# A one-core hybrid encoder layer: PSUM scaling of q and k on VectorE, h stored as two parts, roots of the later blocks beside the gate/up products, larger early weight rings

## The chip, the core and the metric

The kernel runs on one core of a Trainium2 chip. The metric is the device time of one launch in microseconds; the time of a kernel is the median of its runs. The engines are PE (TensorE, matrix products), DVE (VectorE), ACT (ScalarE), POOL (GpSimd) and SP (SyncE). SP issues nearly all DMA transfers, and it does so in the order of its queue: a transfer whose data are not ready holds up all transfers behind it.

## The reference

One layer over 2048 prompt rows and 8 streams of 16 rows (2176 rows in all), model width 1024, FFN width 2816, all in float32:

```python
h = _rmsnorm(x, norm1_g) * (1 + scale) + shift
z = h @ w_in                                  # 1024 -> 2568 columns
u_a, u_g, q, k, v, f = jnp.split(z, ...)
u = u_a * jax.nn.sigmoid(u_g)
q = _rmsnorm(q.reshape(b, t, N_HEADS, HEAD_DIM), q_norm_g)
k = _rmsnorm(k.reshape(b, t, N_HEADS, HEAD_DIM), k_norm_g)
logf = jax.nn.log_sigmoid(f + b_f)
...
attn = softmax(q k / 8 + cum[q] - cum[k], causal) @ v
conv_out = silu(layernorm(causal_depthwise_conv31(u) + conv_b))
x = x + g1 * (concat(conv_out, attn) @ w_out)
h = _rmsnorm(x, norm2_g) * (1 + sc2) + sh2
x = x + g2 * ((jax.nn.silu(h @ w_gate) * (h @ w_up)) @ w_down)
```

The outputs are x, the normed k, v, logf and the last convolution rows.

## The kernel before

Activations lie with channels on the 128 partitions and rows of the sequence along the free axis. A float32 product is made from parts: each factor is split into a high part (rounded to the fp32r format by ACT, "Copy") and a low part (the factor less its high part, a subtraction on DVE or POOL), and PE runs three matmuls, high with high, low with high, high with low. So each operand of a product costs an ACT pass and a subtraction, and a tile is ready for PE when both are done.

The program is written as Python code for each stage, and a planner of the framework puts the instructions of each engine into a fixed order by a simulation of its own. All engines then run their own lists in order and wait for each other by semaphores. A list that is ordered badly for the real durations stands still behind the instruction that waits.

The stages that the change touches:

- **u and v** (`project_u_v`, blocks of 384 rows). `h_block` makes the normed input h for a block: for each of 8 channel tiles SP loads xT, POOL multiplies by the root (L464), ACT scales and shifts (L466), SP writes h to memory (`h_d`, L471), ACT and POOL make its parts `hh` and `hl` (L472, L473). Three buffers hold h, 16 each hold the parts.
- **q and k** (`project_q_k`). For each block, `load` reads h back and makes its parts a second time (L501 to L503). `product` makes 8 products of 24 matmuls (L514), 4 for q and 4 for k; ACT copies each out of PSUM and squares it. `finish` for the block before is woven in, one step per product: the head sums, a root by Newton steps on DVE (L94 to L96), and then for each of 8 tiles a matmul that spreads the root over the channels (`R`, L549), and the scaled q or k. For rows below `LATE = 1536` ACT scales R by the gain (L553) and POOL multiplies (L554); for later rows DVE does both in one instruction that reads R from PSUM (L556). Then the parts of the result are made on ACT (L559) and POOL (L560) and written out by SP (`q_d`, `k_d`, `o_k`, L563 to L566).
- Beside it run the depthwise convolution (`conv_taps`, 31 taps, L706 on DVE, 7 chunks of rows) and the remaining modulation vectors (`ada_rest`: a load `wa` into a single buffer, L266, matmuls L271, then L279 on DVE). A chunk of the convolution accumulates in two PSUM banks (`cv`) up to row 1536, and in SBUF (`ca`) for the later chunks.
- **Attention** follows, with the last of the finishing work, the convolution's normalization and the sample streams.
- **Output projection** (`project_out`, 6 blocks of 360 or 368 rows). For each block 8 tiles `cr` are loaded (three buffers), split into `ch` (ACT) and `cl` (POOL, L1141) and multiplied with w_out (L1124) into 8 PSUM banks; `scaled_add` adds the result to x; the squares are summed in `ssum` on POOL. `root` takes the root of the mean of squares: four matmuls (L1171), a chain of 16 short DVE instructions, four matmuls (L1180), an ACT copy. The root of a block is taken in the block after; those of blocks 2 to 5 are written to `r_d`. After block 2, `norm(0)` makes the normed inputs of the first pair of blocks: 16 multiplies on POOL (L1245), 16 on ACT (L1247), sums and differences on DVE (L1285), and writes to `ht_d`.
- **Gate/up and down products** (`ffn_up`, `ffn_down`). A scheme of seven products per pair of blocks takes the place of eight. Weights W and right sides T go through rings of slots: raw weights `rR` (512 columns each), split weights `rW`, split right sides `rT`. For the first pair of blocks the sums of weights are made on DVE (L1352) as well. `pump` issues loads and splits until the rings are full; `rings` opens small rings (8 T, 4 W, 4 R) before the output projection, `grow` opens the rest after it (R 11, W 6, T 13 and 9). A product takes four T and one W: 12 matmuls (L1424). `norms` makes the normed inputs of pairs 1 and 2 beside the products of pair 0, one step after every second product. PSUM banks go round in the order of `BANK8`, where bank `ss` is every eighth.

Of the kernel before, what the change touches and what calls it, by code (L numbers as in the profile page):

```python
# [43 lines left out]
LATE = 1536  # L44
# [74 lines left out]
class Layer:  # L119
# [30 lines left out]
    def run(self, stop=99):  # L150
# [3 lines left out]
        with ExitStack() as ctx:  # L154
# [5 lines left out]
            self.h_d = d.tile([P, CB, TT], F32, name="h_d")  # L160
# [269 lines left out]
    def h_block(self, b0, b1, xp, sp, hp, ep=None):  # L430
# [44 lines left out]

    def project_q_k(self):
# [49 lines left out]
        def finish(b0, b1, zs, ss, sqs, tag):  # L526
# [16 lines left out]
            for g in range(NP):  # L543
                for w in range(2):
# [7 lines left out]
                    if b0 < LATE:  # L552
                        nc.scalar.activation(y[:, :n], R, AF.Copy, scale=self.gain[:, w, g:g + 1])  # L553
                        nc.gpsimd.tensor_tensor(y[:, :n], zs[w][g][:, :n], y[:, :n], ALU.mult)  # L554
                    else:
                        nc.vector.scalar_tensor_tensor(y[:, :n], zs[w][g][:, :n], self.gain[:, w, g:g + 1], R, ALU.mult, ALU.mult)  # L556
# [119 lines left out]
    def conv_taps(self, ch):  # L676
# [5 lines left out]
        for jp in range(2):  # L682
# [468 lines left out]
    def project_out(self, ctx):  # L1151
# [3 lines left out]
        ones = sp.tile([P, P], F32, name="ones2")  # L1155
        nc.vector.memset(ones, 1.0)
        mean = sp.tile([P, 2], F32, name="mean2")
        nc.vector.memset(mean, 1.0 / D)
        ident = sp.tile([P, P], F32, name="ident2")
        nc.sync.dma_start(ident, a["ident"])  # L1160
# [478 lines left out]
```

## Time and profile before

| what | value |
|---|---|
| median of 3 runs | 2921.28 us (2919.7 to 2922.06) |
| the profiled execution | 2918.41 us, of which 2916.6 us is the span from its first to its last instruction |
| mean granted TensorE clock | 0.965 |
| PE busy | 2743.4 us, 94% of the span |
| DVE busy | 2163.8 us, 74% |
| ACT, POOL busy | 1469.7 us (50%), 681.7 us (23%) |
| DMA | 585.43 MB, mean 201 GB/s |

The profile counts an engine as busy from the start to the end of its instructions. A line of a table of stretches gives for each engine the busy time and, in brackets, the number of instructions, then the clock that was granted to TensorE (1.00 is full speed), the share of time that the 16 DMA engines were busy, and GB/s. In a list of groups the last two numbers before the second bar are the total busy time and the mean ns of one instruction. "[14.77 <-DMA wa<-w_ada]" behind an instruction says that its engine stood idle for 14.77 us before it, until that transfer landed. A row with "x32" merges 32 instructions, and its second number is then the time from the start of the first to the end of the last.

### The profile page before, as it was taken

What the parts mean: (1) busy time and instruction counts of PE and PEld (TensorE: products, weight loads), DVE (VectorE), ACT (ScalarE), POOL (GpSimd) and SP (SyncE); (2) the same over time, 40 slices, a digit from 0 to 9 for tenths busy, and PEclk for the clock granted to TensorE, in tenths of its full rate; (3) what the DMA queues carried; (4) which work ended last, traced back from release to release, by engine and by line L of the source; (5) the groups of instructions that cost most, each with busy time, mean ns of one, the idle gap of its engine ahead of it and who ended that gap; (6) DMA issues with size and microseconds to landing.
All of it is one profiled execution on the core that took longest, in us unless ns stands there. A gap on an engine that the chain in (4) does not pass through costs nothing.

```text
span 2916.6 us, 48768 instructions
## 1 busy us (share of the span) xinstructions
PE 2743.4 (94%) x16536; PEld 2530.6 (87%) x16536; DVE 2163.8 (74%) x4155; ACT 1469.7 (50%) x2892; POOL 681.7 (23%) x813
## 2 busy tenths in 40 slices
PE   7999989789899899989879999999999999999999
PEld 6999967666566677779878999999999999999999
DVE  3698988878778677742349999877797778676765
ACT  4533424346676667764335444544454446555553
POOL 3555555553222223225524200000000000000000
PEclk9999999898998999999989999999999999999999
DMA  8643536464333866453638877867696678888883
GB/s 300 223 132 110 163 122 193 137 186 133 95 94 113 193 191 186 146 179 124 218 124 287 299 246 233 276 216 224 219 314 201 207 226 274 266 258 270 271 261 116
DMA packets 377738, 585.43 MB, mean 201 GB/s; under 512 B 46240, under 2 KB 236864, under 8 KB 375440
## 3 DMA queue, kind: packets, MB, share of 16 engines
q1 hardware_dynamic: 363024, 556.89, 59.6%
q0 software_dynamic: 14464, 25.42, 3.7%
q8 instruction: 131, 2.15, 0.3%
q14 instruction: 119, 0.97, 0.1%
HBM read 413.05 MB, written 169.16 MB: 200 GB/s over the span
## 4 chain that ended last, share of the span: by engine, by line
PE 55%; DVE 4%; DMA 3%; ACT 1%; issue 1%; POOL 1%; SPq 0%; DVEq 0%; POOLq 0%; ACTq 0%
PE z L1424 41%; PE acc L1124 6%; PE pv L948 3%; PE s L957 1%; PE s L958 1%; DVE rW L1141 1%; PE mx L918 1%; PE lane L1087 1%; DVE rR L1352 1%; DMA nx<-x_d 1%; POOL nx L1245 1%; DMA rR<-w_up 1%; PE lane L1053 1%; DMA vraw<-o_v 0%; PE pr L1180 0%
## 5 line engine op out<-in xcount | busy, mean ns | idle before, releaser
L1424 PE MATMUL z<-rT,rW 128*128 128x360 f32 (+1 forms) x8316 | 1379.2, 328 | 19.1 <-ACT rW L1140 15.6
L1424 PEld LDWEIGHTS z<-rT,rW 128*128 128x128 f32 x8316 | 1376.5, 188 | 21.3 <-ACT rW L1140 17.0
L1140 ACT ACTIVATE rW<-rR 128x512 fp32r<-128x512 f32 x714 | 433.7, 616 | 373.5 <-PE z L1424 272.3
L1141 DVE TENSOR_TENSOR rW<-rR,rW 128x512 fp32r<-128x512 f32 x714 | 482.2, 680 | 140.0 <-ACT rW L1140 135.5
L948 PE MATMUL pv<-e,V 128*128 128x512 f32 (+3 forms) x960 | 268.3, 384 | 3.9 <-DVE e L1141 1.1
L706 DVE SCALAR_TENSOR_TENSOR cv<-cu,cpar,cv 128x384 f32<-128x384 f32 x464 | 248.8, 614 | 4.7 <-ACT cv L704 4.4
L921 DVE TENSOR_REDUCE M<-mx 128x1 f32<-128x512 f32 (+2 forms) x320 | 189.3, 604 | 62.2 <-PE mx L918 41.8
L962 ACT ACTIVATE ef<-s 128x512 f32<-128x512 f32 (+3 forms) x320 | 165.9, 531 | 120.2 <-PE s L958 43.5
L948 PEld LDWEIGHTS pv<-e,V 128*128 128x128 f32 x960 | 169.7, 194 | 52.5 <-DVE e L1141 6.1
L1141 POOL TENSOR_TENSOR e<-ef,e 128x512 fp32r<-128x512 f32 (+3 forms) x106 | 126.6, 1194 | 376.3 <-ACT e L1140 179.6
L1141 DVE TENSOR_TENSOR rT<-traw,rT 128x360 fp32r<-128x360 f32 (+1 forms) x315 | 160.0, 540 | 68.9 <-ACT rT L1140 68.7
L1140 ACT ACTIVATE rT<-traw 128x360 fp32r<-128x360 f32 (+1 forms) x315 | 148.7, 501 | 93.6 <-DMA traw<-gt_d 71.4
L1141 DVE TENSOR_TENSOR e<-ef,e 128x512 fp32r<-128x512 f32 (+3 forms) x214 | 151.2, 714 | 43.4 <-ACT e L1140 42.0
L1140 ACT ACTIVATE e<-ef 128x512 fp32r<-128x512 f32 (+3 forms) x320 | 174.4, 566 | 5.4 <-PE pv L948 1.0
L918 PE MATMUL mx<-K,Q 96*128 96x512 f32 (+2 forms) x320 | 135.5, 431 | 15.0 <-DVE M L921 14.5
L1124 PE MATMUL acc<-ch,woh 128*128 128x360 f32 (+1 forms) x384 | 128.5, 337 | 12.6 <-ACT ch L1140 10.4
L706 DVE SCALAR_TENSOR_TENSOR ca<-cu,cpar,ca 128x384 f32<-128x384 f32 (+1 forms) x232 | 125.6, 611 | 12.8 <-ACT ca L704 12.7
L514 PE MATMUL z<-hqh,wqh 128*128 128x384 f32 (+1 forms) x384 | 132.3, 345 | 1.3 <-ACT sq L518 1.1
L1352 DVE TENSOR_TENSOR rR<-rR 128x512 f32<-128x512 f32 (+1 forms) x136 | 93.1, 700 | 52.2 <-DMA rR<-w_down 40.1
L957 PE MATMUL s<-Q,K 128*128 128x512 f32 (+3 forms) x320 | 128.5, 403 | 2.5 <-ACT ef L962 2.3
L1124 PE MATMUL acc<-cl,woh 128*128 128x360 f32 (+1 forms) x384 | 120.5, 338 | 10.2 <-POOL cl L1141 10.2
L514 PE MATMUL z<-hql,wqh 128*128 128x384 f32 (+1 forms) x384 | 128.7, 336 | 0.0
(318 smaller groups left out, 4511.7 us busy)
## 6 DMA issues: line engine op xcount, KB each, us to landing
rR<-sup_d SPq DMA_DIRECT2D x176, 256.0 KB
rR<-w_gate SPq DMA_DIRECT2D x132, 256.0 KB
traw<-gt_d SPq DMA_DIRECT2D x154, 180.0 KB
rR<-w_down SPq DMA_DIRECT2D x104, 256.0 KB
rR<-sdn_d SPq DMA_DIRECT2D x96, 256.0 KB
rR<-w_up SPq DMA_DIRECT2D x88, 256.0 KB
sup_d<-rR SPq DMA_DIRECT2D x88, 256.0 KB
wa<-w_ada SPq DMA_DIRECT2D x16, 1024.0 KB
```

The source lines that it names most:

```text
L514: nc.tensor.matmul(z[:, :n], w[:, m], x[:, :n], start=(c == 0 and k == 0), stop=(c == CB - 1 and k == 2))
L706: self.pin(nc.vector.scalar_tensor_tensor(dst, src, w, acc[i], ALU.mult, ALU.add))
L918: nc.tensor.matmul(mx[:, :w], Q2[0:AUX, h, j * P:(j + 1) * P], K2[kb][0:AUX, h, :w], start=True, stop=not diag)
L921: nc.vector.tensor_reduce(M[:, i, kb:kb + 1], mx[:, :w], AX.X, ALU.max)
L948: nc.tensor.matmul(z[h][:, off:], V[kt // 4][:, v, kt % 4, h:h + 2, :].rearrange("p b c -> p (b c)"), e[:, x, off:], start=(kt == 0 and i ...
L957: nc.tensor.matmul(s[:, off:], K1[kb][:, h, sl], Q1[:, h, off:], start=True, stop=False)
L962: nc.scalar.activation(ef[:, off:], s[:, off:], AF.Exp)
L1124: self.nc.tensor.matmul(z[:, :n], w[:, m], y, start=(first and i == 0 and k == 0), stop=(last and i == len(terms) - 1 and k == 2))
L1140: self.nc.scalar.activation(hi, raw, AF.Copy)
L1141: engine.tensor_tensor(lo, raw, f32(hi), ALU.subtract)
L1352: nc.vector.tensor_tensor(t, x, y, op)
L1424: nc.tensor.matmul(z, W[:, x, m], t[:, y, :w], start=(k == 0 and i == 0), stop=(k == n - 1 and i == 2))
```

## The change

1. DVE scales every tile of q and k out of PSUM in one instruction; the branch with ACT and POOL is gone.
2. `h_d` holds both parts of h, so the q and k stage loads them ready to use; the write waits for the low part, and twice as many bytes go each way.
3. The chunk of the convolution that ends at row 1920 accumulates in PSUM as well.
4. In the output projection the low parts `cl` are made by DVE, `cr` has four buffers, and `pump` is called once before the last block.
5. `root` becomes a method that two stages call. For blocks 2 to 5 the output projection writes the sums of squares to `r_d`, and `norms` takes the root beside the gate/up products, in PSUM bank `ss`.
6. The early rings are larger (W 6, R 12); the sum is W 10 as before, R 15 as before, T 29 (30 before).

```diff
-LATE = 1536
...
-            self.h_d = d.tile([P, CB, TT], F32, name="h_d")
+            self.h_d = d.tile([P, CB, 2, TT], F32, name="h_d")
...
-            hl = hp.tile([P, NB], F32R, tag="hl", name="hl")
-            hh = hp.tile([P, NB], F32R, tag="hh", name="hh")
+            hx = hp.tile([P, 2, NB], F32R, tag="hx", name="hx")
+            hh, hl = hx[:, 0], hx[:, 1]
...
-            nc.sync.dma_start(self.h_d[:, c, b0:b1], h[:, :n])
             nc.scalar.activation(hh[:, :n], h[:, :n], AF.Copy)
             nc.gpsimd.tensor_tensor(hl[:, :n], h[:, :n], f32(hh[:, :n]), ALU.subtract)
+            nc.sync.dma_start(self.h_d[:, c, :, b0:b1], f32(hx[:, :, :n]))
             yield hh, hl
...
-                h = hp.tile([P, NB], F32, tag="h", name="hq", bufs=3)
-                nc.sync.dma_start(h[:, :n], self.h_d[:, c, b0:b1])
-                nc.scalar.activation(hh[:, :n], h[:, :n], AF.Copy)
-                nc.gpsimd.tensor_tensor(hl[:, :n], h[:, :n], f32(hh[:, :n]), ALU.subtract)
-                hs.append((hh, hl))
+                hx = hp.tile([P, 2, NB], F32R, tag="hx", name="hqx")
+                nc.sync.dma_start(f32(hx[:, :, :n]), self.h_d[:, c, :, b0:b1])
+                hs.append((hx[:, 0], hx[:, 1]))
...
-                    if b0 < LATE:
-                        nc.scalar.activation(y[:, :n], R, AF.Copy, scale=self.gain[:, w, g:g + 1])
-                        nc.gpsimd.tensor_tensor(y[:, :n], zs[w][g][:, :n], y[:, :n], ALU.mult)
-                    else:
-                        nc.vector.scalar_tensor_tensor(y[:, :n], zs[w][g][:, :n], self.gain[:, w, g:g + 1], R, ALU.mult, ALU.mult)
+                    nc.vector.scalar_tensor_tensor(y[:, :n], zs[w][g][:, :n], self.gain[:, w, g:g + 1], R, ALU.mult, ALU.mult)
...
-            if c1 <= 1536:
+            if c1 <= 1920:
                 acc = [shaped(self.bank("cv", "cv")) for _ in range(2)]
...
-                raw = cp.tile([P, NW], F32, tag="cr", name="cr")[:, :n]
+                raw = cp.tile([P, NW], F32, tag="cr", name="cr", bufs=4)[:, :n]
...
-                self.parts_of(hh, hl, raw, nc.gpsimd)
+                self.parts_of(hh, hl, raw, nc.vector)
...
-            if b1 == TT:
-                self.pump()
...
-            if pending:
-                R = root(*pending)
-                if bi < 3:
-                    first.append(R)
-                if bi == 2:
-                    drain(self.norm(0, sp, lambda k, h: xs01[h][k], first))
+            if 0 < bi < 3:
+                first.append(self.root(*pending, sp))
+            if bi == 2:
+                drain(self.norm(0, sp, lambda k, h: xs01[h][k], first))
             if bi < 2:
                 xs01 = (xs01 if bi else []) + [xs]
-            pending = (bi, ssum)
-        root(*pending)
+                pending = (ssum, n)
+            else:
+                nc.sync.dma_start(self.r_d[bi, :, :n], ssum[:, :n])
+            if bi == len(HALVES) - 2:
+                self.pump()
...
-                r = pool.tile([P, NW], F32, tag="nR", name="nR", bufs=2)
-                nc.sync.dma_start(r[:, :n], self.r_d[2 * p + h, :, :n])
-                R.append(r)
+                s = pool.tile([P, NW], F32, tag="ns", name="ns", bufs=1)
+                nc.sync.dma_start(s[:, :n], self.r_d[2 * p + h, :, :n])
+                R.append(self.root(s, n, pool))
+                yield
...
-        for k, n in (("T", 8), ("W", 4), ("R", 4)):
+        for k, n in (("T", 8), ("W", 6), ("R", 12)):
...
-        for k, n, side in (("R", 11, None), ("W", 6, "right"), ("T", 13, "right"), ("T", 9, None)):
+        for k, n, side in (("W", 4, "right"), ("T", 16, "right"), ("R", 3, None), ("T", 5, None)):
```

The body of `root` is as before; its constants now live in a pool of their own that `rings` opens.

Because the planner orders the engines anew, the places that matter are shown as the lists have them. The lines after the change have other numbers (L706 is L697, L1141 is L1132, L1424 is L1412, L1171 and L1180 are L1203 and L1212).

First DVE in the q and k stage, while the chunk of rows 1536 to 1920 is convolved (`ca` and `cv` are its accumulators, `qn` the scaled q or k, `mod` the modulation vectors). Before:

```order
L706 SCALAR_TENSOR_TENSOR ca<-cu,cpar,ca 128x384 x2
L282 TENSOR_SCALAR mod_108<-mod_108,n2T 128x9
L706 SCALAR_TENSOR_TENSOR ca<-cu,cpar,ca 128x384 x32
L279 TENSOR_SCALAR mod_106<-pm_4967,bT 128x9
L279 TENSOR_SCALAR mod_107<-pm_4967,bT 128x9
```

After:

```order
L697 SCALAR_TENSOR_TENSOR cv<-cu,cpar,cv 128x384 x7
L547 SCALAR_TENSOR_TENSOR qn<-zs,gain,R 128x384
L697 SCALAR_TENSOR_TENSOR cv<-cu,cpar,cv 128x384 x8
L547 SCALAR_TENSOR_TENSOR qn<-zs,gain,R 128x384
L697 SCALAR_TENSOR_TENSOR cv<-cu,cpar,cv 128x384 x9
L547 SCALAR_TENSOR_TENSOR qn<-zs,gain,R 128x384
```

The run of 32 convolution steps without a break is cut into runs of 8 with one `qn` between, and its accumulator is in PSUM.

Then PE at the start of the gate/up products (`acc` is the last block of the output projection, `z` the gate/up products, 12 matmuls each, `pr` the two matmul groups of a root). Before:

```order
L1124 MATMUL acc<-cl,woh 128x360
L1424 MATMUL z<-rT,rW 128x368 x30
L1171 MATMUL pr<-mean_13543,ssum 90x2 x4
L1424 MATMUL z<-rT,rW 128x368 x18
L1180 MATMUL pr<-odg,ones_13541 128x90 x4
L1171 MATMUL pr<-mean_13543,ssum 90x2 x4
L1180 MATMUL pr<-odg,ones_13541 128x90 x4
L1424 MATMUL z<-rT,rW 128x368 x1800
```

After:

```order
L1115 MATMUL acc<-cl,woh 128x360
L1412 MATMUL z<-rT,rW 128x368 x264
L1203 MATMUL pr<-sp_13266,ns 90x2 x4
L1412 MATMUL z<-rT,rW 128x368 x72
L1212 MATMUL pr<-odg,sp_13265 128x90 x4
L1203 MATMUL pr<-sp_13266,ns 90x2 x4
L1212 MATMUL pr<-odg,sp_13265 128x90 x4
L1412 MATMUL z<-rT,rW 128x368 x372
L1203 MATMUL pr<-sp_13266,ns 90x2 x4
L1412 MATMUL z<-rT,rW 128x368 x90
```

The root of block 4 and that of block 5 stood 30 and 48 matmuls into the gate/up products; now 22 products come first, then the root of block 2, with 6 products between its two groups, and right behind it the root of block 3 with nothing between; those of blocks 4 and 5 follow further down with products between.

DVE at the same place (`xo` is x after the projection, `rT` and `rW` the low parts of right sides and weights, `rR` sums of weights, `ov`, `or`, `ot` and `odg` the chain of a root, `e` and `eU` the first results that are taken out of the gate/up products). Before:

```order
L1141 TENSOR_TENSOR rT<-traw,rT 128x368
L1136 TENSOR_TENSOR xo<-xo,acc 128x128
L1141 TENSOR_TENSOR rT<-traw,rT 128x368 x8
L1173 TENSOR_SCALAR ov<-pr 90x4
L1141 TENSOR_TENSOR rT<-traw,rT 128x368
L1174 TENSOR_SCALAR or<-ov 90x4
L1141 TENSOR_TENSOR rT<-traw,rT 128x368
L1175 TENSOR_SCALAR or<-or 90x4
L1141 TENSOR_TENSOR rT<-traw,rT 128x368
L94 SCALAR_TENSOR_TENSOR ot<-or 90x4
L1141 TENSOR_TENSOR rT<-traw,rT 128x368
L95 TENSOR_TENSOR ot<-ot,ov 90x4
```

After:

```order
L1123 SCALAR_TENSOR_TENSOR xo<-acc,mod_106,xo 128x232
L1127 TENSOR_TENSOR xo<-xo,acc 128x128
L1340 TENSOR_TENSOR rR<-rR 128x512 x3
L1126 TENSOR_TENSOR acc<-acc,mod_106 128x128
L1132 TENSOR_TENSOR rW<-rR,rW 128x512
L1340 TENSOR_TENSOR rR<-rR 128x512
L1132 TENSOR_TENSOR rW<-rR,rW 128x512
L1132 TENSOR_TENSOR rT<-traw,rT 128x368 x3
L1127 TENSOR_TENSOR xo<-xo,acc 128x128
L1132 TENSOR_TENSOR rT<-traw,rT 128x368 x3
L1132 TENSOR_TENSOR rW<-rR,rW 128x512 x6
L1132 TENSOR_TENSOR rT<-traw,rT 128x368 x4
```

The low parts of right sides were alternated with a root's chain and no weight was made; now sums and low parts of weights alternate with right sides, and of the first weights six are made ahead of the last `xo` where it was four.

Last SP in the u and v stage, where the parts of h are made for a block (`h` is the tile that xT is loaded into). Before:

```order
L345 DMA o_v<-v 128x252
L471 DMA h_d<-h 128x384 x2
L345 DMA o_v<-v 128x260
L463 DMA h<-xT 128x384
L345 DMA o_v<-v 128x252
L463 DMA h<-xT 128x384 x2
L471 DMA h_d<-h 128x384 x3
```

After:

```order
L344 DMA o_v<-v 128x252
L437 DMA x<-x 128x1024 x2
L344 DMA o_v<-v 128x260
L344 DMA o_v<-v 128x252
L472 DMA h_d<-hx 128x2x384
L462 DMA h<-xT 128x384
L472 DMA h_d<-hx 128x2x384
```

Writes and loads went in groups of up to three; now each load of the next tile stands behind a write that waits for a low part.

More of the change, by code (lines that the diff above doesn't have):

```diff
@@ L1154, in project_out @@
         sp = ctx.enter_context(self.pool(name="osp", bufs=1))
[L1155 to L1160, printed above, removed]
         self.tables("silu_and_others", self.last_exp)
@@ L1163, in project_out @@
         W = {}
-        def root(bi, ssum):
-            n = HALVES[bi][1] - HALVES[bi][0]
-            m = n // 4
-            pr = self.bank("ss", "pr")
-            for i in range(4):
-                nc.tensor.matmul(pr[:m, 2 * i:2 * i + 2], ssum[:, i * m:(i + 1) * m], mean, start=True, stop=True)
-            v, r, t = (sp.tile([P, 4], F32, tag=k, name="o" + k)[:m] for k in "vrt")
-            nc.vector.tensor_scalar(v, pr[:m, 0:8:2], EPS, None, ALU.add)
-            nc.vector.tensor_scalar(r.bitcast(I32), v.bitcast(I32), 1, None, ALU.arith_shift_right)
-            nc.vector.tensor_scalar(r.bitcast(I32), r.bitcast(I32), -1, 0x5F3759DF, ALU.mult, ALU.add)
-            newton_rsqrt(nc, r, t, v, 3)
-            for i in range(4):
-                dg = sp.tile([P, NW // 4], F32, tag="dg", name="odg", bufs=4)[:m, :m]
-                nc.vector.tensor_scalar(dg, ident[:m, :m], r[:, i:i + 1], None, ALU.mult)
-                nc.tensor.matmul(pr[:, i * m:(i + 1) * m], ones[:m], dg, start=True, stop=True)
-            R = sp.tile([P, NW], F32, tag="R", name="oR", bufs=2)
-            nc.scalar.copy(R[:, :n], pr[:, :n])
-            if bi < 2:
-                return R
-            nc.sync.dma_start(self.r_d[bi, :, :n], R[:, :n])
         pending, first = None, []
@@ L1291, in rings @@
         self.count = dict.fromkeys("TWR", 0)
-        for k, n in (("T", 8), ("W", 4), ("R", 4)):
+        for k, n in (("T", 8), ("W", 6), ("R", 12)):
             self.slots(ctx, k, n)
+        cp = ctx.enter_context(self.pool(name="spread", bufs=1))
+        self.spread = ones, mean, ident = [cp.tile([P, k], F32, name=f"sp{i}") for i, k in enumerate((P, 2, P))]
+        self.nc.vector.memset(ones, 1.0)
+        self.nc.vector.memset(mean, 1.0 / D)
+        self.nc.sync.dma_start(ident, self.a["ident"])
         self.tr = ctx.enter_context(self.pool(name="traw", bufs=6))
```

20 lines of the change are left out of this document (18 added, 2 removed).

## The prediction

> **What bounds the kernel now.** I read the table of stretches first, cut where PE changes its work: u and v, q and k, attention, output projection, start of the gate/up products, the rest.
>
> ```profile
> 0.00:344.30 344.30, 319.62 (x2304) 311.50 (x2305) 252.50 (x518) 142.89 (x264) 166.87 (x323) 0.98 0.56 183
> 344.30:645.30 301.00, 260.04 (x1498) 217.29 (x1496) 257.81 (x544) 120.50 (x257) 179.82 (x179) 0.94 0.54 161
> 645.30:1271.80 626.50, 573.07 (x3173) 416.18 (x3172) 467.05 (x809) 428.47 (x859) 177.48 (x175) 0.93 0.50 143
> 1271.80:1500.40 228.60, 205.50 (x1216) 203.59 (x1217) 78.25 (x175) 91.58 (x172) 101.71 (x103) 0.94 0.52 170
> 1500.40:1713.40 213.00, 186.40 (x1090) 183.55 (x1089) 191.94 (x373) 100.06 (x196) 55.81 (x36) 0.93 0.81 274
> 1713.40:2916.60 1203.20, 1198.74 (x7260) 1198.48 (x7260) 916.23 (x1741) 586.15 (x1147) 0.00 (x0) 1.00 0.75 239
> ```
>
> PE (first pair of numbers) is the bound nearly everywhere. The last row has no gap, and nothing in the change makes its matmuls fewer. What can be won are the gaps of the rows between: 41 us in q and k, 23 in the output projection, 27 at the start of gate/up, and the slow clock behind each gap. So next I read what PE waited for there.
>
> ```profile
> PE pm L271 <- DMA wa<-w_ada: 16.3, 2, 14.8
> PE R L549 <- DVE mod L279: 11.4, 3, 6.2
> PE acc L1124 <- ACT ch L1140: 10.4, 2, 8.3
> PE acc L1124 <- POOL cl L1141: 10.2, 2, 5.8
> PE ssq L523 <- ACT sq L518: 10.0, 2, 8.7
> ```
>
> The longest wait names a DMA; the timeline tells why that transfer was late.
>
> ```profile
> 411.33 17.02 DVE L706 SCALAR_TENSOR_TENSOR ca<-cu,cpar,ca 128x384 f32<-128x384 f32 x32
> 412.02 17.18 POOL L560 TENSOR_TENSOR qp<-qn,qp 128x384 fp32r<-128x384 f32 x1 [0.64 <-ACT qp L559]
> 430.65 0.54 SPq L266 DMA_DIRECT2D wa<-w_ada  x1
> 437.98 1.94 PE L271 MATMUL pm<-wa,sT 128*32 128x512 f32 x8 [14.77 <-DMA wa<-w_ada]
> 522.52 13.70 POOL L554 TENSOR_TENSOR qn<-zs,qn 128x384 f32<-128x384 f32 x1 [4.72 <-ACT qn L553]
> 536.25 0.52 ACT L559 ACTIVATE qp<-qn 128x384 fp32r<-128x384 f32 x1 [13.81 <-POOL qn L554]
> ```
>
> While DVE ran 32 convolution steps with all operands in SBUF, one POOL subtraction took 17.18 us; SP stood behind it with the writes of q, and the load `wa` behind those. At 522 the same befell L554, ACT stood behind it, and PE behind ACT's squares (the 8.7 us).
>
> **Scaling on DVE, and one more chunk in PSUM.** The rows for the prices:
>
> ```profile
> L560 POOL TENSOR_TENSOR qp<-qn,qp 128x384 fp32r<-128x384 f32 (+1 forms) x48 | 70.9, 1478 | 65.7 <-ACT qp L559 65.6
> L554 POOL TENSOR_TENSOR qn<-zs,qn 128x384 f32<-128x384 f32 x32 | 57.2, 1788 | 46.3 <-ACT qn L553 46.2
> L556 DVE SCALAR_TENSOR_TENSOR qn<-zs,gain,R 128x384 f32<-128x384 f32 (+1 forms) x16 | 8.6, 540 | 9.2 <-DMA o_k<-qn 4.9 <-POOL qp L560 2.7 <-PE R L549 0.9
> 392.00:453.00 61.00, 35.73 (x58) 0.86 0.44 141
> 453.00:505.00 52.00, 45.39 (x52) 1.00 0.68 206
> 173.28 7.44 DVE L706 SCALAR_TENSOR_TENSOR cv<-cu,cpar,cv 128x384 f32<-128x384 f32 x14
> 360.00:422.90 62.90, 53.51 (x291) 49.57 (x289) 1.00 0.38 128
> ```
>
> The two stretches in the middle count the convolution (L706) alone, the last one the matmuls L514. DVE gains 32 instructions of 0.540 us, 17.3 us. The moved chunk took 35.73 + 45.39 = 81.1 us for 110 steps; into PSUM a step takes 7.44/14 = 0.53 us, so 58.3, 22.8 less. DVE's sum goes from 257.8 to 252.3 us in a stretch of 301. PE without waits made 291 matmuls in 62.9 us, 0.216 each; 960 of that size and 192 of 256 columns (two thirds each, estimated) are 235 us, and some 10 for the first attention matmuls in the last block: 245. Both engines thus want about 250, and each waits for the other once per product (R for DVE, banks for PE). I add a tenth, 275: **26 us won**. Ends: 255 (46 won) if they never wait, 301 (none) if DVE's rows, now 4.8 us per product with one `qn` behind 8 steps, hold PE's R banks each time. POOL's 57.2 us go, and its L560 waits at most for a run of 8 steps in PSUM. The later chunks, 128 columns wide, stay in SBUF, in runs of up to 16 between two `qn`: short stops of POOL remain.
>
> **Parts of h stored.** In q and k, 48 ACT copies and 48 POOL subtractions go; PE's list names them with 0.3 us only, so I give nothing for them beyond the above. Each way 128 x 8 x 2176 x 4 bytes, 8.9 MB, are added: 30 GB/s on 161 in q and k, where the DMA engines are busy 54% of the time, hidden. In u and v it is 26 on 183. There the first block's 1.6 MB come while weights are awaited; at 300 GB/s (slice 1 of the page) they last 5 us. I take 2 lost, ends 0 and 5, and nearer the low end since the writes stand behind the loads in SP's order.
>
> **Output projection.** The rows:
>
> ```profile
> 1280.00:1500.40 220.40, 200.06 (x1152) 196.84 (x1152) 0.95 0.52 169
> 1400.25 8.97 POOL L1245 TENSOR_TENSOR xo<-xo,oR 128x368 f32<-128x368 f32 x8 [3.04 <-ACT oR L1182]
> 1410.47 2.77 PE L1124 MATMUL acc<-cl,woh 128*128 128x360 f32 x8 [5.84 <-POOL cl L1141]
> 1404.66 1.30 DVE L1285 TENSOR_TENSOR ot<-xo 128x368 f32<-128x368 f32 x1
> 1414.71 0.53 DVE L1285 TENSOR_TENSOR ot<-xo 128x368 f32<-128x368 f32 x1
> 1418.76 0.91 SPq L1199 DMA_DIRECT2D cr<-cat_d  x2
> L1180 PE MATMUL pr<-odg,ones 90*128 90x90 f32 (+1 forms) x48 | 8.2, 327 | 7.3 <-DVE odg L1179 7.3
> L1171 PE MATMUL pr<-mean,ssum 128*90 128x2 f32 (+1 forms) x48 | 5.0, 226 | 0.6 <-ACT oR L1182 0.6
> ```
>
> 1152 matmuls at 1198.74/7260 = 0.165 us are 190 us; 220 were spent. PE stood behind POOL's `cl` for 10.2 us, because 8 multiplies `xo` stood ahead of it. Then a `cr` load stood on SP behind the writes of `ht_d` until 1418.76. The first stop goes with `cl` on DVE, which is busy 78 us of 228.6 here and takes on 48 x 0.54 = 26 us; the second goes by the fourth buffer and the order, in which block 3's tiles are loaded ahead of the writes. Slow clock behind both, about 4. The root of block 2 and that of block 3 leave: (8.2 + 5.0)/6 = 2.2 us of PE each. And ACT makes the first `ch` ahead of four copies `rW`, 4 x 0.62 = 2. In all 10 + 3 + 4 + 4 + 2 = 23, less 7 for stops that the new order brings: **16 us won**, ends 3 (only the roots) and 23. The summing on POOL stays and is off PE's path; if it ran late it would hold `ssum`, and so the root of the next block only.
>
> A rule of the Trainium skill speaks here. The row first: DVE's L1285 took 1.30 us beside POOL's multiplies and 0.53 without. The Trainium skill (SBUF — State Buffer, section "Who interferes with whom") states that a DVE instruction with two inputs in SBUF contends with a POOL instruction that reads SBUF, and that one of them blocks fully. By that, 411 to 428 us was such a stop and PSUM accumulators end it, but `cl` on DVE is now one more such instruction beside `xo` and `ssum`. That is the second rival.
>
> **Roots beside gate/up, more weights ready.**
>
> ```profile
> 1500.40:1550.00 49.60, 20.47 (x101) 18.88 (x102) 0.69 0.66 214
> 1550.00:1650.00 100.00, 100.00 (x601) 100.00 (x601) 1.00 0.90 306
> 1650.00:1713.40 63.40, 59.98 (x357) 59.12 (x356) 1.00 0.80 269
> 1516.32 1.37 PE pr L1171 x8
> 1520.36 2.03 PE pr L1180 x8
> 1522.41 0.47 ACT oR L1182
> 1523.26 4.46 DMA rR<-w_up
> ```
>
> These stretches count L1424 alone, the four rows below are from the chain of waits. 1059 matmuls at 100/601 = 0.166 are 176 us; 213 passed. Two roots stood in line, then the load of `w_up` began only at 1523. Now six weights and 12 raw ones are there before, so 8 T and 6 W carry PE over the first 6 products at least in W, and no root comes before product 22. What is late next: DVE, 191.9 us busy of 213. It gains two roots, 2 x 16 x 0.2 = 6.4, and loses two `rW` and four `rR`, 2 x 0.68 + 4 x 0.70 = 4.2 (0.68 and 0.70 from the groups of L1141 and L1352): 194. PE needs 176, four roots of 2.2, and for block 3's root, which has nothing between its groups, DVE's chain from 1517.69 to 1520.36, 2.7, and ACT's 0.47: 188. DVE is the bound; with 6 for waits 200: **13 us won**, ends 3 and 19. One T less ahead costs nothing, since behind 1713 PE never waited for T.
>
> **The sum.** 26 + 16 + 13 - 2 = 53. The profiled execution took 2918.4, so 2865; the median stood 2.9 above it: 2868 us.
>
> **Rivals.** (A) DVE's list, with `qn` in it, becomes the bound of q and k and PE waits for R at each product: only 5 of the 26 are left, 2868 + 21 = 2889. For it: 252 us of DVE against 245 of PE. Against it: the planner's even spacing. (B) By the mechanism of the 1.30 us row, `cl` waits on DVE behind stretched L1285, and PE again behind `cl`; and the roots' chain stands in a DVE list that has no slack: 14 and 10 less, 2892. (C) Slower: in u and v each load of xT stands on SP behind a write that waits for the low part, 0.50 (ACT) and 0.99 (POOL) later than before. A tile may take 344.3/48 = 7.2 us; its chain is 1.01 + 0.67 + 0.50 + 0.99 = 3.2 with three buffers. Only if waits bring a tile over 7.2 does it decide, and then 48 x 1.49 = 72 us are lost against the sum: 2940.
>
> ```profile
> L464 POOL TENSOR_TENSOR h<-h,R 128x384 f32<-128x384 f32 (+1 forms) x48 | 47.9, 1013 | 57.9 <-DMA h<-xT 26.7 <-ACT R L457 21.4 <-issue 7.0
> ```
>
> (0.67, 0.50 and 0.99 are the means of L466, L472 and L473 in the same list.) (D) Everything goes to its floor, 46 + 23 + 19: 2833. (E) The planner orders attention anew; it has 53 us of gaps in 626, and were they doubled the gain would be gone: 2921.
>
> **Chances.** Forecast 0.54, A 0.16, B 0.10, D 0.10, E 0.05, C 0.05. A measurement here tells about 0.2% (6 us) from no change. So faster 0.90, same 0.05, slower 0.05. The range 2836 to 2900 takes in A and B, and most of D; the forecast's own is 2855 to 2882.
>
> **What would show it.** Right: no POOL instruction over 6 us in q and k; the q and k matmuls done in 265 to 285 us; no wait of `acc` for `cl` over 2 us; L1412 (once L1424) with over 130 matmuls more in its first 50 us, and one gap of some 3 us at the second root. Wrong: waits of R for `qn` that add up to over 20 us (A), waits of `acc` for DVE (B), gaps of PE before 344 us (C), or attention longer than 626 us (E).

## The result, and the profile after

The median is 2841.7 us (2837.6 to 2850.5), against 2921.5 us for the kernel before in the same comparison: a ratio of 0.9732, 95% interval 0.9709 to 0.9755. The profiled execution has a span of 2839.3 us, 77.3 less than before. The time lies inside the forecast's range (2836 to 2900) but outside the likeliest case's own (2855 to 2882): the gain is 80 us, not 53. All medians and ratios leave out three runs that took 17 to 95% longer than their fellows: one of e3, one of e7 and one of the kernel before in the comparison of e5 to e8.

The table of stretches of the kernel after, cut at the first matmul of q and k, their last, the first of the output projection and the first of gate/up (the sixth row begins behind the last of the four roots):

```profile
0.00:350.10 350.10, 323.33 (x2306) 314.17 (x2306) 252.67 (x515) 141.09 (x257) 163.53 (x319) 0.98 0.63 208
350.10:600.40 250.30, 250.05 (x1490) 210.21 (x1491) 232.41 (x571) 84.62 (x176) 58.83 (x101) 1.00 0.70 222
600.40:1219.10 618.70, 565.53 (x3180) 414.51 (x3179) 476.49 (x827) 436.76 (x876) 179.71 (x176) 0.93 0.50 146
1219.10:1432.60 213.50, 202.72 (x1184) 200.16 (x1185) 95.14 (x189) 84.85 (x163) 56.40 (x55) 0.97 0.58 192
1432.60:1640.00 207.40, 194.87 (x1149) 192.45 (x1148) 184.59 (x388) 101.40 (x196) 32.01 (x28) 0.96 0.74 248
1640.00:2839.30 1199.30, 1194.85 (x7235) 1194.39 (x7233) 916.68 (x1751) 588.13 (x1146) 12.75 (x8) 1.00 0.76 243
```

For two of the cuts the prediction's rows of before end elsewhere (1271.8 is the end of PE's last work ahead of the output projection, 1280 the start of its first product). With the same cuts as above the rows of before read:

```profile
645.30:1280.00 634.70, 573.07 (x3173) 416.18 (x3172) 472.34 (x819) 436.51 (x873) 177.48 (x175) 0.92 0.50 143
1280.00:1500.40 220.40, 205.50 (x1216) 203.59 (x1217) 72.96 (x166) 83.54 (x158) 101.71 (x103) 0.95 0.52 169
```

| stage | before | after | measured | forecast |
|---|---|---|---|---|
| u and v | 344.3 | 350.1 | +5.8 | +2 |
| q and k | 301.0 | 250.3 | -50.7 | -26 |
| attention, with the gap at its end | 634.7 | 618.7 | -16.0 | 0 (2 of the 16 below lie in its gap) |
| output projection | 220.4 | 213.5 | -6.9 | -16 |
| from the first gate/up product on | 1416.2 | 1406.7 | -9.5 | -13 |
| span | 2916.6 | 2839.3 | -77.3 | -53 |

In the second row PE is busy for 250.05 of 250.30 us at clock 1.00. The list of waits of PE in that stretch is two lines, where before it had 14.8 us behind a load and 8.7 behind the squares:

```profile
PE z L509 <- DVE logf L346: 0.8, 1, 0.8
PE pcum L615 <- POOL logf L608: 0.3, 1, 0.3
```

The longest POOL instruction left in q and k, with the DVE rows round it (timelines of POOL and of DVE):

```profile
565.74 3.92 POOL L551 TENSOR_TENSOR qp<-qn,qp 128x384 fp32r<-128x384 f32 x1 [4.47 <-ACT qp L550]
...
565.02 3.24 DVE L697 SCALAR_TENSOR_TENSOR ca<-uS,cpar,ca 128x128 f32<-128x128 f32 x12
568.17 0.61 DVE L697 SCALAR_TENSOR_TENSOR cu<-uS,cpar,ca 128x128 f32<-128x128 f32 x2
568.69 0.61 DVE L547 SCALAR_TENSOR_TENSOR qn<-zs,gain,R 128x384 f32<-128x384 f32 x1
```

POOL's subtraction stands from 565.74 until DVE has left its run of SBUF steps and `qn`, which reads PSUM, comes; POOL is done 1 us after `qn` began. Before, the same kind of instruction stood for 17.18 us beside 32 steps that nothing parted.

### The profile page after: what moved, and what is told of

It reads as the page before. It is cut to its first block, busy times and chain, and to the rows that moved or that the text cites. A ratio compares the mean times of both kernels' runs of the same rounds, so it can differ in the third digit from the quotient of the medians.

```text
span 2839.3 us, 48486 instructions
## 1 busy us (share of the span) xinstructions
PE 2731.4 (96%) x16536; PEld 2525.9 (89%) x16536; DVE 2158.0 (76%) x4235; ACT 1436.9 (51%) x2812; POOL 503.2 (18%) x685
## 4 chain that ended last, share of the span: by engine, by line
PE 78%; DMA 9%; DVE 5%; issue 4%; ACT 2%; POOL 1%; SPq 1%; POOLq 0%; ACTq 0%; DVEq 0%
PE z L1412 44%; PE z L509 7%; PE pv L939 5%; PE acc L1115 4%; PE pa L319 3%; PE pvv L339 3%; PE pg L319 3%; PE s L948 2%; PE s L949 2%; PE mx L909 2%; DMA vraw<-o_v 1%; DVE M L912 1%; DMA k_d<-qp 1%; PE pu L319 1%; DMA wraw<-w_in 1%
## 5 line engine op out<-in xcount | busy, mean ns | idle before, releaser
L1412 PE MATMUL z<-rT,rW 128*128 128x360 f32 (+1 forms) x8316 | 1382.0, 328 | 4.3 <-ACT oR L1214 2.0
L1412 PEld LDWEIGHTS z<-rT,rW 128*128 128x128 f32 x8316 | 1378.9, 188 | 5.9 <-ACT oR L1214 2.4
L1132 DVE TENSOR_TENSOR rW<-rR,rW 128x512 fp32r<-128x512 f32 x714 | 480.7, 678 | 150.5 <-ACT rW L1131 147.3
L697 DVE SCALAR_TENSOR_TENSOR cv<-cu,cpar,cv 128x384 f32<-128x384 f32 x580 | 311.7, 618 | 2.0 <-ACT cv L695 1.6
L509 PE MATMUL z<-hqx,wqh 128*128 128x384 f32 (+1 forms) x768 | 196.5, 333 | 0.8 <-DVE logf L346 0.8
L1132 DVE TENSOR_TENSOR rT<-traw,rT 128x360 fp32r<-128x360 f32 (+1 forms) x315 | 158.6, 537 | 44.9 <-ACT rT L1131 44.6
L1132 POOL TENSOR_TENSOR e<-ef,e 128x512 fp32r<-128x512 f32 (+3 forms) x106 | 128.1, 1209 | 361.8 <-ACT e L1131 170.5
L1132 DVE TENSOR_TENSOR e<-ef,e 128x512 fp32r<-128x512 f32 (+3 forms) x214 | 147.9, 701 | 42.9 <-ACT e L1131 41.6
L509 PEld LDWEIGHTS z<-hqx,wqh 128*128 128x128 f32 x768 | 135.7, 188 | 18.7 <-issue 15.5
L1115 PE MATMUL acc<-ch,woh 128*128 128x360 f32 (+1 forms) x384 | 122.6, 338 | 16.1 <-ACT ch L1131 8.2
L1115 PE MATMUL acc<-ch,wol 128*128 128x360 f32 (+1 forms) x384 | 127.7, 336 | 0.0
L509 PE MATMUL z<-hqx,wql 128*128 128x384 f32 (+1 forms) x384 | 126.4, 329 | 0.0
```

Source lines behind the costliest of these rows:

```text
L509: nc.tensor.matmul(z[:, :n], w[:, m], x[:, :n], start=(c == 0 and k == 0), stop=(c == CB - 1 and k == 2))
L697: self.pin(nc.vector.scalar_tensor_tensor(dst, src, w, acc[i], ALU.mult, ALU.add))
L1115: self.nc.tensor.matmul(z[:, :n], w[:, m], y, start=(first and i == 0 and k == 0), stop=(last and i == len(terms) - 1 and k == 2))
L1132: engine.tensor_tensor(lo, raw, f32(hi), ALU.subtract)
L1412: nc.tensor.matmul(z, W[:, x, m], t[:, y, :w], start=(k == 0 and i == 0), stop=(k == n - 1 and i == 2))
```

## The experiments

All kernels with their stages in us, cut as above, each from one profiled execution; medians and ratios are from the timed runs, each ratio against runs of the kernel before on the same chip. The medians of before in the three comparisons were 2920.0 (e1 to e4), 2916.9 (e5 to e8) and 2915.1 (e9 to e12), so kernels of different comparisons are set side by side by their ratios. For e7 there are no stages; e9 is the same kernel again, with them.

| kernel | u, v | q, k | attention | out | gate/up on | median | ratio (95%) |
|---|---|---|---|---|---|---|---|
| before | 344.3 | 301.0 | 634.7 | 220.4 | 1416.2 | 2921.5 | 1 |
| after | 350.1 | 250.3 | 618.7 | 213.5 | 1406.7 | 2841.7 | 0.9732 (0.9709 to 0.9755) |
| e1 front only | 351.5 | 250.2 | 625.5 | 219.9 | 1417.7 | 2862.4 | 0.9814 (0.9784 to 0.9843) |
| e2 after, old scaling | 348.3 | 260.6 | 628.3 | 208.9 | 1407.0 | 2855.0 | 0.9801 (0.9758 to 0.9845) |
| e3 after, chunk in SBUF | 351.9 | 250.0 | 614.3 | 206.8 | 1407.9 | 2832.8 | 0.9707 (0.9672 to 0.9742) |
| e4 after, h whole | 345.1 | 255.2 | 616.0 | 209.5 | 1411.3 | 2836.6 | 0.9721 (0.9690 to 0.9752) |
| e5 before, new scaling | 345.0 | 267.2 | 627.6 | 219.3 | 1416.8 | 2875.2 | 0.9852 (0.9809 to 0.9895) |
| e6 before, chunk in PSUM | 346.5 | 264.2 | 623.8 | 219.3 | 1416.3 | 2884.0 | 0.9883 (0.9844 to 0.9923) |
| e7 before, h as parts | | | | | | 2891.8 | 0.9922 (0.9893 to 0.9951) |
| e9 the same | 353.5 | 281.4 | 624.8 | 219.9 | 1414.3 | 2899.4 | 0.9948 (0.9930 to 0.9966) |
| e8 after, roots in line | 349.7 | 250.4 | 622.3 | 220.7 | 1416.1 | 2857.0 | 0.9795 (0.9765 to 0.9825) |
| e10 after, `cl` on POOL | 351.6 | 249.5 | 621.0 | 222.7 | 1411.0 | 2856.9 | 0.9809 (0.9792 to 0.9825) |
| e11 after, small early rings | 347.0 | 250.4 | 618.0 | 207.2 | 1417.5 | 2843.8 | 0.9763 (0.9746 to 0.9780) |
| e12 three edits | 344.3 | 249.9 | 615.7 | 212.8 | 1410.6 | 2835.2 | 0.9730 (0.9716 to 0.9744) |

**e1: the front of the program alone.** The kernel after up to attention, the kernel before from `project_out` on.

> The kernel after with the output projection, the roots, the rings and the norms of the kernel before: only scaling on DVE, h stored as parts and the moved chunk are left. In the comparison of the two traces u and v cost 5.7 us, q and k won 50.7, attention with the gap at its end won 16.3, and the rest won 16.3 more. If attention's gain belongs to the front of the program: 2921.5 + 5.7 - 50.7 - 16 = 2860. If it was only another order that the planner found because the later stages changed: 2876, with attention (to the first matmul of the output projection) near 635 again.

Measured 2862.4, so near the 2860 of the first case. The parts add up: the front wins what it wins in the kernel after, and the back is at its old 219.9 and 1417.7. Attention lies between, 9 us shorter than before and 7 longer than after.

**e2: q and k of the earlier rows scaled by ACT and POOL again**, with the other parts of the change kept:

```diff
-                    nc.vector.scalar_tensor_tensor(y[:, :n], zs[w][g][:, :n], self.gain[:, w, g:g + 1], R, ALU.mult, ALU.mult)
+                    if b0 < 1536:
+                        nc.scalar.activation(y[:, :n], R, AF.Copy, scale=self.gain[:, w, g:g + 1])
+                        nc.gpsimd.tensor_tensor(y[:, :n], zs[w][g][:, :n], y[:, :n], ALU.mult)
+                    else:
+                        nc.vector.scalar_tensor_tensor(y[:, :n], zs[w][g][:, :n], self.gain[:, w, g:g + 1], R, ALU.mult, ALU.mult)
```

> The kernel after with q and k of rows below 1536 scaled by ACT and POOL again. Theory 1 (the stops came from POOL being locked out behind convolution steps with all operands in SBUF): the chunk stays in PSUM, so POOL's 57 us do no harm, q and k stay under 260 us and the time is 2842 to 2850. Theory 2 (the chain of ACT and POOL itself was too long for the banks of R): waits of R return, q and k take 270 or more, the time is 2860 to 2870.

q and k take 260.6, just over theory 1's bound and well under theory 2's; the total of 2855 lies between the two. POOL's timeline has longer stops again, though none of 17 us:

```profile
500.71 7.73 POOL L549 TENSOR_TENSOR qn<-zs,qn 128x384 f32<-128x384 f32 x1 [3.81 <-ACT qn L548]
523.84 6.51 POOL L549 TENSOR_TENSOR qn<-zs,qn 128x384 f32<-128x384 f32 x1 [3.58 <-ACT qn L548]
```

They fall into the chunks of 128 columns, which still accumulate in SBUF; the two stood beside runs of 37 and 24 steps of DVE. PE's waits in the stage add up to 7.0 us, 1.9 of them for `wa`.

**e3: the chunk that ends at row 1920 in SBUF again.**

```diff
-            if c1 <= 1920:
+            if c1 <= 1536:
```

> The kernel after with the chunk that ends at row 1920 accumulated in SBUF again. Theory 1: POOL's L551 is stopped in runs of 8 steps (6 us), and DVE's list grows by 23 us from 232 to 255 in a stage of 250, so it becomes the bound: q and k take 260 to 275, the time is 2852 to 2867. Rival (POOL has no more work there that matters, and DVE has slack): same as after, 2842.

The rival is right: q and k take 250.0, and the total is no worse than after (0.9707, the intervals overlap). The row of the 384-column steps that accumulate in SBUF, from the groups of DVE in q and k, of the kernel before and then of e3, shows what the prediction had wrong about their price:

```profile
L706 DVE SCALAR_TENSOR_TENSOR ca<-cu,cpar,ca 128x384 f32<-128x384 f32 x116 | 84.5, 796 | 0.3 <-ACT ca L704 0.3
```

```profile
L697 DVE SCALAR_TENSOR_TENSOR ca<-cu,cpar,ca 128x384 f32<-128x384 f32 x116 | 68.9, 658 | 0.0
```

The same 116 steps in the same memory went from 84.5 to 68.9 us, with 67 us of POOL work beside them instead of 180. PSUM would make it some 62 (0.53 each). The place of the accumulators had no price of its own: with no POOL instruction beside it a step in SBUF took 0.61 us from start to end in both kernels, as it does in PSUM (0.62), and the 32 steps at 411.33 in the prediction's timeline took 17.02 us, 0.53 each. What the prediction priced at 22.8 us was contention with POOL, and two thirds of it go with POOL's work alone.

**e4: h stored whole and split again in q and k** (the part of the diff on `h_d` undone).

> The kernel after with h stored as one float32 tensor and split again in the q and k stage. u and v return to 344, 6 us less. If the second making of the parts cost nothing in q and k (the prediction's view): q and k stay at 250 and the time is 2836. Rival (48 copies of ACT and 48 subtractions of POOL stood in lists that PE waited for): q and k take 265 to 275, the time is 2851 to 2861.

u and v are back at 345.1, q and k 5 us longer, the total 2836.6: the prediction's view holds, with a small price of the second splitting (`wa` waits once for 3.5 us).

**e5, e6, e7: each of the three front parts alone, in the kernel before.** The edits are those of the diff: the branch `if b0 < LATE` gone (e5), `c1 <= 1920` (e6), `h_d` with two parts (e7).

> The kernel before with one edit: DVE scales every tile of q and k out of PSUM. In DVE's list each qn now parts the convolution: runs of ca steps are at most 8 (384 columns) and 15 (128 columns), where they were 32 and 43. Theory 1 (POOL stands still for as long as DVE runs steps with all operands in SBUF, so the length of the runs decides): no POOL instruction over 6 us, q and k 252 to 262 us, total 2868 to 2880. Theory 2 (POOL and ACT simply had too much work in the stage, 180 us of POOL, and each part of the change takes some away): POOL goes from 180 to 123, a bit under half of the way, q and k near 278, total near 2899.

> The kernel before with one edit: the chunk that ends at row 1920 accumulates in PSUM. Theory 1: the runs of 31 and 32 are gone, those of 34, 37 and 43 steps of 128 columns (12 to 15 us each) stay: the stop of 17.2 us at 412 and the late load behind it go, the later ones stay, q and k 275 to 288, total 2895 to 2908. Theory 2: POOL's work is unchanged, q and k 295 to 301, total 2915 to 2921.

> The kernel before with one edit: h stored as two parts. POOL loses 46 us of work in q and k, ACT some 25, but runs of 28, 35 and 43 steps stay in DVE's list. Theory 1: POOL still stops for 15 us and more, q and k 288 to 301, u and v 350, total 2914 to 2927. Theory 2: q and k near 280, total near 2906.

Each alone is faster than before, by 1.5, 1.2 and 0.8% (0.5% in e9), with intervals that leave out 1. For e5 theory 1 gives the total (2875 in 2868 to 2880) and POOL's longest instructions, `hql` with 4.99 and `qp` with 4.96 us; but q and k took 267.2, 5 more than it allowed, since the loads `wa` were still late and cost PE 8.3 us. For e6 theory 1 has the direction, but it won more than that allowed: 264.2 in the profile (of an execution 12 us below the median of the runs) and 2884 in the median. The stop of 17.18 us is gone there, and with it the wait for `wa` (16.3 us in PE's list before, none in e6). The longest POOL instruction, 9.27 us from 497.95 on, lies beside a run of 37 steps of 128 columns that DVE began at 496.02 and left at 505.82. For e7 theory 1 said no gain, and that is wrong; theory 2's total, near 2906, is too high as well.

**e9: the last one again, for its profile.**

> The same kernel as the run with only h stored as two parts, for a profile to be read; its time was 2896, so some 27 us come out of q and k or attention against 6 lost in u and v. Theory 1 (runs of 28, 35 and 43 convolution steps still stop POOL): a POOL instruction of 13 us or more is still there, but PE's wait behind it is shorter than 14.8, because the q and k writes on SP or the copies on ACT have fewer neighbours; q and k 275 to 285. Theory 2 (POOL's amount of work was the cause): no POOL instruction over 9 us, q and k 270 to 280.

The timelines of DVE and POOL, then two rows of PE's list of waits:

```profile
414.63 18.62 DVE L702 SCALAR_TENSOR_TENSOR ca<-cu,cpar,ca 128x384 f32<-128x384 f32 x35
```

```profile
419.56 14.53 POOL L550 TENSOR_TENSOR qn<-zs,qn 128x384 f32<-128x384 f32 x1 [46.20 <-ACT qn L549]
```

```profile
PE ssq L519 <- ACT sq L514: 9.2, 1, 9.2
PE R L545 <- ACT qn L549: 8.0, 2, 7.3
```

As theory 1 had it here: the run of 35 steps holds POOL until it ends, at 433.25 (POOL at 434.09), but PE's waits are 7 and 9 us instead of 15, and q and k take 281.4. It is likely, but not shown, that the stop costs less because POOL has less to do ahead of it and behind it. The length of the run alone does not make a stop, though. In the kernel before, the next run of this length, 31 steps, has 15 POOL instructions inside it, none over 1.4 us (timelines of DVE and of POOL):

```profile
483.07 27.84 DVE L706 SCALAR_TENSOR_TENSOR ca<-cu,cpar,ca 128x384 f32<-128x384 f32 x31
...
490.28 3.90 POOL L503 TENSOR_TENSOR hql<-hq,hqh 128x384 fp32r<-128x384 f32 x3
494.13 1.33 POOL L560 TENSOR_TENSOR qp<-qn,qp 128x384 fp32r<-128x384 f32 x1
```

There DVE paid: a step beside which POOL had its turn took 1.36 us instead of 0.61, and the run 27.84 us for 31 steps where the one at 411 took 17.02 for 32. So the length of a run bounds how long POOL can stand, the work behind it sets what that costs, and what decides whether POOL stands or gets its turn stays open. The gains alone are 33.8, 36.8 and 19.6 us in q and k, 90 together, and the three at once won 50.7: a wait can be won only once.

**e8: all roots in the output projection again, with the large rings.**

```diff
-            if 0 < bi < 3:
-                first.append(self.root(*pending, sp))
+            if pending:
+                R = self.root(*pending, sp)
+                if bi < 3:
+                    first.append(R)
+                else:
+                    nc.sync.dma_start(self.r_d[bi - 1, :, :pending[1]], R[:, :pending[1]])
...
+            if b1 == TT:
+                R = self.root(*pending, sp)
+                nc.sync.dma_start(self.r_d[bi, :, :n], R[:, :n])
```

> The kernel after with the roots of all blocks taken in the output projection again (the large rings stay). The prediction's view: the output projection costs 4 us more (two roots at 2.2 us of PE), and the roots of blocks 4 and 5 stand early in the gate/up products with stalls of 4.3 and 2.7 us of which PE had as many with the roots at the later place: 2841.7 + 4 to 8 = 2846 to 2850. Rival (the rings are the whole gain; a root costs the same wherever it stands): 2842.

15 us slower than after, more than forecast: 7.2 in the output projection and 9.4 from the first gate/up product on. PE, at the root of block 4, now waits for a chain of 16 short steps that stand one by one among splits and sums of weights in DVE's full list. PE's row, then the first and the last of the chain's steps in DVE's timeline:

```profile
1471.12 1.16 PE L1217 MATMUL pr<-odg,sp 90*128 90x90 f32 x4 [12.37 <-DVE odg L1216]
```

```profile
1457.02 0.15 DVE L1210 TENSOR_SCALAR ov<-pr 90x4 f32<-90x4 f32 x1
1457.09 0.97 DVE L1132 TENSOR_TENSOR rT<-traw,rT 128x368 fp32r<-128x368 f32 x2
1457.99 0.68 DVE L1132 TENSOR_TENSOR rW<-rR,rW 128x512 fp32r<-128x512 f32 x1
...
1470.80 0.79 DVE L1216 TENSOR_SCALAR odg<-sp,or 90x90 f32<-90x90 f32 x4
```

**e10: `cl` on POOL again.**

```diff
-                self.parts_of(hh, hl, raw, nc.vector)
+                self.parts_of(hh, hl, raw, nc.gpsimd)
```

> The kernel after with the low parts cl of the output projection on POOL again. The prediction's view: PE waits behind the POOL multiplies xo for cl again, 10 us: the output projection takes 220 to 225 instead of 213.5, the total is 2850 to 2855. Rival (DVE's list holds cl up as much as POOL's did, since the run with the roots in line had cl on DVE and took 220.7): 207 to 214, total 2835 to 2842.

The prediction's view: the output projection takes 222.7 us, 9.2 more, the total of 2856.9 is 2 above the range, and the wait is back (PE's list of waits):

```profile
PE acc L1115 <- POOL cl L1132: 11.6, 4, 6.2
```

**e11: the early rings of the kernel before** (one T less in the last ring, since the constants of `root` need the room).

```diff
-        for k, n in (("T", 8), ("W", 6), ("R", 12)):
+        for k, n in (("T", 8), ("W", 4), ("R", 4)):
...
-        for k, n, side in (("W", 4, "right"), ("T", 16, "right"), ("R", 3, None), ("T", 5, None)):
+        for k, n, side in (("R", 11, None), ("W", 6, "right"), ("T", 13, "right"), ("T", 8, None)):
```

> The kernel after with the early rings of the kernel before (W 4, R 4; the later slots W 6, R 11, T 13 and 8). The prediction's view: the first weights come late as before, PE waits some 9 and 6 us for them with slow clock behind: the part from the first gate/up product on takes 1416 to 1424 instead of 1406.7, total 2851 to 2859. Rival (the run with the roots in line had the large rings and took 1416.1 there, as before, so the place of the roots is the whole gain): 1407, total 2842.

The stage does what the prediction said (1417.5, with a wait of 9.03 us for the first weights), but the total is only 0.3% above after. The output projection took 207.2, 6.3 less. In the kernel after, PE waits there for the high parts `woh` of w_out (a row of its list of waits, then the table of the stretch); in e11 no such wait is left:

```profile
PE acc L1115 <- ACT woh L1131: 4.5, 3, 2.4
```

```profile
1212.00:1250.00 38.00, 28.42 (x151) 27.19 (x150) 19.58 (x35) 21.59 (x37) 0.00 (x0) 0.87 0.94 329
```

Eight loads of raw gate/up weights, 256 KB each, are issued among w_out's between 1216 and 1246, with the DMA engines busy 94%. So part of what the large rings win later may be paid here, but that is not shown: of the kernels with large rings e8, e10 and e12 wait 4.2 to 4.7 us for `woh`, while e2, e3 and e4 wait only 1.0 to 1.2 and their output projection, 206.8 to 209.5 us, is about as short as e11's.

**e12: three edits to the kernel after**: the chunk in SBUF (e3), four buffers for h in u and v, and `root` written as steps that the weaving of `norms` takes one at a time:

```diff
-            h = (ep or hp).tile([P, NB], F32, tag="h", name="h", bufs=4 if ep else 3)
+            h = (ep or hp).tile([P, NB], F32, tag="h", name="h", bufs=4)
...
             nc.tensor.matmul(pr[:m, 2 * i:2 * i + 2], ssum[:, i * m:(i + 1) * m], mean, start=True, stop=True)
+        yield
...
         newton_rsqrt(nc, r, t, v, 3)
+        yield
...
-                R.append(self.root(s, n, pool))
+                yield from self.root(s, n, pool, R)
```

> The kernel after with three edits: the chunk in SBUF again, h with four buffers in u and v, and root as steps of its own (the matmul groups of the roots of blocks 2 to 5 stand 24, 34, 37 and 19 products of matmuls further apart from each other or from the next, no two groups side by side without products). If the stalls at the roots (3.2, 2.8, 1.7, 1.4 us and the clock of 0.91 behind them) go, the part from the first gate/up product on takes 1399 to 1402; u and v 345 to 348; the rest as with the chunk in SBUF: 2818 to 2828. Rival (the waits move elsewhere, as DVE is full there): 2833, as with the chunk alone.

(The counts of products in that text are wrong: the order has 6, 7, 9 and 3 between the two groups of the four roots.) The gate/up part took 1410.6, no gain: the waits at the roots only moved (PE's timeline):

```profile
1484.47 1.26 PE L1214 MATMUL pr<-odg,sp 90*128 90x90 f32 x8 [3.21 <-DVE odg L1213]
...
1509.38 0.46 PE L1214 MATMUL pr<-odg,sp 90*128 90x90 f32 x2 [1.39 <-DVE odg L1213]
...
1595.77 1.13 PE L1214 MATMUL pr<-odg,sp 90*128 90x90 f32 x8 [2.07 <-DVE odg L1213]
...
1616.74 1.13 PE L1214 MATMUL pr<-odg,sp 90*128 90x90 f32 x8 [1.81 <-DVE odg L1213]
```

The fourth h buffer did what was asked: u and v 344.3. In total 0.9730 against 0.9732 and 0.9707: neither e12 nor e3 is told apart from the kernel after by these runs, though both have the lower medians.

## Why the prediction was right, and where its sizes were off

**q and k, 26 forecast, 50.7 measured.** The mechanism is the one named: POOL stood still beside a DVE run in SBUF, SP and ACT stood behind POOL, PE behind them. e6 shows it most plainly, where one chunk moved to PSUM takes away the longest stop and the wait for `wa`; in e9 the stops stay, and with them PE's waits of 7.3 and 9.2 us behind ACT. The step that failed is "each waits for the other once per product ... I add a tenth, 275". PE's work was priced right (245, measured 250.05), but there was no mutual waiting: PE waited 1.1 us. The reason given, that both lists want about 250 us, was wrong on DVE's side: its list took 232.4 us, not 252.3. `qn` was priced right: the 32 of the stage took 19.5 us, 4 of them already there before (2.4), so 17.1 more for the 17.3 forecast. The rest is that DVE's other steps became shorter when POOL left, also those that were never moved: the 232 steps of 128 columns took 81.2 us before and 71.9 after. A sum of busy time that contains contention is no price of the work. With 18 us of slack in DVE, no `qn` was late.

The Trainium skill (SBUF — State Buffer, section "Who interferes with whom") states that such a DVE instruction contends with POOL's reads. The traces agree (1.36 us for a step of 0.61) and go further on one point: POOL may get no turn between one DVE instruction and the next, but only at the end of a run of 35 (14.53 us) or at a `qn` (3.92 us). Mostly it gets one: of the 205 two-input POOL instructions that began beside such a step with at least 2 us of the run still ahead, in q and k of ten of the kernels, 29 stood until the run ended.

**u and v, 2 forecast, 5.8 measured.** Just over the upper end. It is not the bytes: e12 writes as many and has 344.3 with a fourth h buffer, while the eight profiles with the parts stored and three buffers have 347.0 to 353.5. That points to rival C's mechanism at a fraction of its price: SP's waits with the writes of `h_d` for the low parts add up to 44.4 us in the kernel after and 29.3 in e12. How this reaches PE is not shown, since PE's own waits for `hx` are 9.1 us in the one and 8.7 in the other.

**Output projection, 16 forecast, 6.9 measured and 1.9 in the gap before it.** Three terms came as priced or better. No wait for `cl` is left (10.2 us), and e10 gives 9.2 back for 10. The roots are worth 7.2 in e8 for 4.4. "7 for stops that the new order brings" became 7.4: waits of 4.5 us for `woh` and 2.9 for `xo` on DVE. What failed are two of the smaller terms. The 4 for slow clock did not come: the 1152 products were busy for 200.06 us before and 199.65 after. And the stop behind the `cr` load, priced at 3, did not go, as the order still puts writes of `ht_d` ahead of it on SP until 1365.27 (timelines of SP, ACT and PE):

```profile
1365.27 2.11 SPq L1162 DMA_DIRECT2D cr<-cat_d  x4
```

```profile
1368.98 0.50 ACT L1131 ACTIVATE ch<-cr 128x360 fp32r<-128x360 f32 x1 [9.34 <-DMA cr<-cat_d]
```

```profile
1329.77 0.40 PE L1115 MATMUL acc<-ch,woh 128*128 128x360 f32 x1 [2.26 <-DVE xo L1123]
...
1369.54 0.43 PE L1115 MATMUL acc<-ch,woh 128*128 128x360 f32 x1 [1.87 <-ACT ch L1131]
```

The stop of this kind before was 2.10 us long, so 0.2 was won.

**Gate/up, 13 forecast, 9.5 measured.** L1412 made 292 matmuls in its first 50 us where L1424 made 101, so the start is as forecast. The first two roots cost a gap each, where one gap was forecast (3.20 and 2.79 us), and in that stretch of 50 us the granted clock was 0.83:

```profile
1482.60:1532.60 50.00, 41.45 (x221) 40.12 (x221) 38.48 (x89) 21.32 (x40) 13.71 (x12) 0.83 0.73 241
```

That rings and roots need each other was not said: with either put back (e11, e8) the stage takes 1416 to 1418, all of its gain gone, while the six kernels that have both take 1407 to 1411.

**Attention, nothing forecast, 16.0 measured.** This is the term that was missing. In every kernel with any part of the front it took 614 to 628 us against 634.7; in the five with the front of the kernel after and its chunk in PSUM (after, e1, e8, e10, e11) 618 to 626. PE's idle time in it fell from 61.6 to 53.2 us, and its busy time by 7.5. Two waits of before are smaller, 4.6 us for a `qn` on DVE (now 1.4) and 5.9 for a load `cy` (now 2.6). Since each part alone brings 7 to 11 us, and every edit orders the stage anew, which of them is cause and which is luck of the order stays open; only that the front carries some 9 of it is shown, by the one profile of e1. Without these 16 us the span would have fallen by 61 instead of 77, inside the likeliest case's own range, and that too by luck, since q and k won 25 more than forecast where the other three stages fell 16 short of it.

**The rivals.** A did not happen (DVE had slack). B's first half did not (no wait for `cl` on DVE), its second half did: the chain of a root stands in a full DVE list. D came nearest to the number, but by another way: q and k went below its floor of 255, attention helped, and the other stages stayed above theirs. E had the right stage and the wrong sign.

## What to carry to other kernels

Look in DVE's list for long runs of instructions with all operands in SBUF while POOL has work: POOL may stand still until the run ends, and whoever waits for POOL with it. It need not, so look at the lengths of POOL's own instructions too. One instruction that reads PSUM every 8 steps or so kept the stops under 5 us here (e5). Do not price work by a busy time that was measured under contention, and do not add up gains that close the same wait. Where an early prefetch and a later consumer were both changed, test each with the other put back: here neither was worth anything from the first gate/up product on without the other.

## What was not expected of the hardware

Every kernel has a stop of PE of 5 to 11 us in the middle of attention (10.7 before, 10.6 after, 9.9 in e8, 10.3 in e10), and in the kernel after it goes back to a DMA. In the kernel after, SP issued the write `bias_d` of 4160 KB at 896.63, and the read of it, next on its queue but for two loads, went out only at 921.74; the load of V that ACT wanted at 911.8 had been issued at 899.18 and landed at 924.40. SP's timeline, and ACT's:

```profile
896.63 0.56 SPq L1022 DMA_DIRECT2D bias_d<-bias  x1
899.18 0.38 SPq L883 DMA_DIRECT2D vraw<-o_v  x1
900.82 3.24 SPq L1036 DMA_DIRECT2D kc<-kcT  x1
921.74 0.85 SPq L1028 DMA_DIRECT2D S<-bias_d  x2
```

```profile
924.40 0.63 ACT L1131 ACTIVATE V<-vraw 128x512 fp32r<-128x512 f32 x1 [12.64 <-DMA vraw<-o_v]
```

So a small load (256 KB) took 25 us when it was issued behind one large write, with the DMA engines busy all the while (0.99 or more of every 5 us from 900 to 925). That the write is the cause is not shown, since no run here took it apart or moved it; it is the next thing to try.
